# A two-layer encoder: the priorities of its list scheduler shifted by a table

## The chip, the cores and the metric

The kernel runs on one core of a Trainium2 chip. The core has five engines that run side by side: TensorE (PE, matmuls into PSUM), VectorE (DVE), ScalarE (ACT), GpSimd (POOL) and SyncE (SP, which here issues all DMAs). Each engine works through its own queue strictly in the order written in the program, and waits on semaphores for what the others must have finished. The metric is the device time of one execution in microseconds, lower is better.

## The reference

A bidirectional encoder trunk of two layers on a sequence of 512 tokens of width 1024, all in float32:

```python
h = layer_norm(x, ln_in_g, ln_in_b)
for l in range(2):
    proj = h @ w_in[l]                     # 1024 x 4608, split into nine parts
    # 4 heads of differential softmax attention, partial rotary
    a = softmax(q0 k0) - lam * softmax(q1 k1);  da = rms_norm(a @ v)
    # 4 heads of a gated linear recurrence, one scan per direction, summed
    hg = rms_norm(scan_fwd + scan_bwd) * silu(gate)
    # 4 heads of cross-attention into a memory of 256 tokens
    mx = softmax(q mk) @ mv
    h = layer_norm(alpha * h + concat(da, hg, mx) @ w_out[l])
    u = depthwise_conv3(h @ w_up[l])       # 1024 x 5632
    h = layer_norm(alpha * h + (silu(u_gate) * u_val) @ w_down[l])
```

## The kernel before, in words

**Matmuls in three halves.** Every large matmul is done in float16 with each operand split into a high and a low half: three matmuls per block (high x high, high x low, low x high), accumulated in float32 in PSUM. A weight block of 1 MB is loaded by a DMA, ScalarE squares and sums it (L307), a one-column matmul adds the sum over the partitions (L168, tile `stat`), VectorE makes a power of two from it (L155, L157, L159), ScalarE writes the scaled high half `wh` (L310) and VectorE the low half `wl` (L311). This chain runs 122 times.

**Stages of a layer.** The input projection (L140 is the one line of all matmuls) fills PSUM tiles `mm` (two buffers). Recurrence heads (`hg`) work through nine levels of block sizes: each level makes small matmuls into PSUM tiles `sc` (three buffers), copies them out under a mask on VectorE (L851, tile `hgD`), and multiplies queries and keys by products of the forget gates (L881 and L885). The differential attention (`da`) makes two score tiles in `sc`, takes their negative maximum (L1039, L1040), the exponential on ScalarE (L1042), their weighted difference (L1049 to L1051), and transposes it on TensorE (L513) into `tr` (two buffers). The output projection and the down projection add each finished PSUM block into the residual stream, which lies in four tiles z0 to z3 of 128 tokens (L569); this also frees the `mm` buffer. When a block of z is complete, its layer norm follows: statistics (L227, L229), an inverse root on GpSimd (L231, L232), scale and shift (L280, L281), transposes (L288) and a split into the halves `xh` and `xl` (L293). At the start the input is normalized block by block (L258), transposed (L262) and scaled by ScalarE (L264).

**What sets the order.** The program is built twice. The first time it is only recorded, as a list of 12099 operations with their engines. `extract` works out which operation depends on which. `deadlines` gives each a priority: for TensorE the place in the recorded order, in microseconds of TensorE work; for the others the latest moment at which they may end, worked back from those who need them. `simulate` then plays a list scheduler on modelled durations: an engine that is free takes, of the operations that are ready, the one with the lowest priority number. `make_plan` hands back the order of each engine and the buffer that each tile gets, and the second build writes exactly that order. So one number in the priorities can move many instructions on all engines, while what is computed stays as it was.

## Time and profile before

| what | value |
|---|---|
| time, median of 3 runs | 1492.83 us (1492.78 to 1493.38) |
| time of the profiled execution | 1492.88 us |
| its span, first to last instruction | 1491.1 us |
| instructions | 24496 |
| TensorE busy | 1451.7 us, 97% |
| VectorE busy | 1168.4 us, 78% |
| ScalarE busy | 865.1 us, 58% |
| GpSimd busy | 130.1 us, 9% |
| DMA moved | 141.91 MB, mean 95 GB/s |

Busy is the time in which an engine works on at least one instruction. The difference of a matmul engine's busy time from the span is what it lost. A wait is listed with the engine and line that ended it. L12 is line 12 of the kernel file; tile names in the profile stand without their numbers.

### The profile page before, as it was taken

To read this page: it belongs to the slowest core of one execution; us is meant where nothing else is said; L and a number is where in the kernel's file an instruction comes from. 1 tells how busy PE (TensorE), PEld (TensorE's weight loads), DVE (VectorE), ACT (ScalarE), POOL (GpSimd) and SP (SyncE) were. 2 spreads that over 40 slices of the span, in tenths; PEclk is the share of its full clock that TensorE was granted. 3 is DMA by queue.
4 is the path that set the end of the run, shared out by engine and by line. 5 is a ranking of instruction groups with operands and counts; after the bars stand their busy time and mean duration, and the time that the engine had idled before them with its cause. 6 is when DMAs were issued, how large, how long until landed. Compare 5 with 4: busy or idle time off the path is not lost. (4 is left out here: it accounts for less than half of the span.)

```text
span 1491.1 us, 24496 instructions
## 1 busy us (share of the span) xinstructions
PE 1451.7 (97%) x9978; PEld 811.9 (54%) x9978; DVE 1168.4 (78%) x2242; ACT 865.1 (58%) x1094; POOL 130.1 (9%) x154
## 2 busy tenths in 40 slices
PE   6999999999999999999999999999999999999997
PEld 4566675565564444444487475655656544444443
DVE  7989968978997677666785978789888777566777
ACT  5876655666376556455466656566645656455550
POOL 1001020000111101001000101001001101001011
PEclk9999999999999999999999999999999999999999
DMA  6342111223143323232324202112232323333221
GB/s 238 114 150 86 59 58 59 101 71 101 46 143 114 107 85 113 85 113 96 128 90 140 87 30 86 57 57 77 79 100 85 113 88 118 99 92 114 86 84 57
DMA packets 158171, 141.91 MB, mean 95 GB/s; under 512 B 3302, under 2 KB 139114, under 8 KB 158058
## 3 DMA queue, kind: packets, MB, share of 16 engines
q1 hardware_dynamic: 158058, 140.35, 29.2%
q8 instruction: 78, 1.28, 0.3%
q14 instruction: 35, 0.29, 0.1%
HBM read 138.24 MB, written 2.10 MB: 94 GB/s over the span
## 5 line engine op out<-in xcount | busy, mean ns | idle before, releaser
L140 PEld LDWEIGHTS <-wh 128*128 128x128 f16 x2624 | 251.0, 98 | 237.5 <-issue 3.4
L311 DVE SCALAR_TENSOR_TENSOR wl<-wst,ws,wh 128x2048 f16<-128x2048 f32 x122 | 312.5, 2561 | 52.3 <-ACT wh L310 51.4
L140 PE MATMUL mm<-xh,wl 128*128 128x512 f16 (+1 forms) x832 | 305.3, 367 | 0.6 <-DVE wl L311 0.6
L140 PE MATMUL mm<-xh,wh 128*128 128x512 f16 (+1 forms) x832 | 305.2, 367 | 0.0
L140 PE MATMUL mm<-xl,wh 128*128 128x512 f16 (+1 forms) x832 | 305.0, 367 | 0.0
L307 ACT ACTIVATE wh<-wst 128x2048 bf16<-128x2048 f32 x122 | 232.2, 1903 | 102.4 <-PE stat L168 49.2
L310 ACT ACTIVATE wh<-wst,ws 128x2048 f16<-128x2048 f32 x122 | 243.5, 1996 | 40.1 <-DVE ws L157 19.5
L140 PE MATMUL mm<-wh,t 128*128 128x512 f16 (+1 forms) x768 | 223.5, 370 | 0.0
L140 PEld LDWEIGHTS <-wl 128*128 128x128 f16 x1312 | 128.2, 98 | 123.0 <-DVE wl L311 0.9
L140 PEld LDWEIGHTS <-t 128*128 128x128 f16 x1152 | 110.2, 98 | 121.4 <-issue 0.6
L569 DVE SCALAR_TENSOR_TENSOR z<-mm,inv,z 128x512 f32<-128x512 f32 x176 | 130.2, 745 | 45.9 <-PE mm L140 32.2
L140 PE MATMUL sc<-xl,wh 128*128 128x512 f16 (+1 forms) x416 | 147.5, 355 | 0.0
L140 PE MATMUL sc<-xh,wl 128*128 128x512 f16 (+1 forms) x416 | 147.5, 355 | 0.0
L140 PE MATMUL sc<-xh,wh 128*128 128x512 f16 (+1 forms) x416 | 147.5, 355 | 0.0
L140 PE MATMUL mm<-wl,t 128*128 128x512 f16 (+1 forms) x384 | 142.1, 370 | 0.0
L155 DVE TENSOR_SCALAR we<-stat 128x1 int32<-128x1 int32 x122 | 18.6, 153 | 118.8 <-PE stat L168 118.6
L1151 POOL TENSOR_TENSOR t<-f 128x512 f32<-128x512 f32 x44 | 60.6, 1378 | 542.7 <-DVE f L1149 438.6
L140 PE MATMUL mm<-wh,mgh 128*128 128x512 f16 x192 | 73.3, 382 | 4.7 <-DVE z L569 4.7
L1147 ACT ACTIVATE f<-sc,cvb,cw 128x512 f32<-128x512 f32 x44 | 34.1, 775 | 71.4 <-PE stat L168 69.3
L140 PE MATMUL mm<-wh,mgl 128*128 128x512 f16 x192 | 72.9, 381 | 0.9 <-DVE mgl L547 0.6
L140 PE MATMUL mm<-wl,mgh 128*128 128x512 f16 x192 | 73.3, 382 | 0.0
L1042 ACT ACTIVATE f<-sc,dam,iqk 128x512 f32<-128x512 f32 x64 | 49.3, 774 | 38.8 <-DVE dam L1040 34.3
(244 smaller groups left out, 2125.4 us busy)
## 6 DMA issues: line engine op xcount, KB each, us to landing
wst<-in_w_up_dram SPq DMA_DIRECT2D x88, 512.0 KB, 4.3
wst<-in_w_in_dram SPq DMA_DIRECT2D x36, 1024.0 KB, 4.8
wst<-in_w_down_dram SPq DMA_DIRECT2D x22, 1024.0 KB, 4.9
wst<-in_w_out_dram SPq DMA_DIRECT2D x12, 1024.0 KB, 4.9
wst<-in_w_mem_kv_dram SPq DMA_DIRECT2D x8, 1024.0 KB, 5.0
z<-in_x_dram SPq DMA_DIRECT2D x4, 512.0 KB, 4.9
mix<-in_ln_g_dram SPq DMA_DIRECT2D x4, 512.0 KB, 3.6
mix<-in_ln_b_dram SPq DMA_DIRECT2D x4, 512.0 KB, 4.7
```

The source lines that it names most:

```text
L140: T.matmul(o, lhsT, rhs, start=start, stop=stop)
L155: V.tensor_scalar(e, tot.bitcast(I32), 0x7F000000, 1, ALU.bitwise_and, ALU.logical_shift_right)
L307: A.activation(h.rearrange("p a b -> p (a b)").bitcast(BF16), flat, AF.Square, accum_out=ss)
L310: A.activation(h.rearrange("p a b -> p (a b)"), flat, AF.Identity, scale=s)
L311: V.scalar_tensor_tensor(l.rearrange("p a b -> p (a b)"), flat, s, h.rearrange("p a b -> p (a b)"), ALU.mult, ALU.subtract)
L569: V.scalar_tensor_tensor(zs, p_, ivs[half % len(ivs)], zs, ALU.mult, ALU.add)
L1042: A.activation(pe[:, c, :], sc_[c], AF.Exp, bias=mx[:, c : c + 1], scale=iqk, accum_out=z1 if c else z0)
L1147: A.activation(c, p_, AF.Identity, scale=cw[:, 1, v : v + 1], bias=cvb[:, l, i + 22 * v : i + 22 * v + 1])
L1151: G.tensor_tensor(gt[:, n, :], c2[:, 0, :], c2[:, 1, :], ALU.mult)
```

## The change

No instruction of the kernel proper is edited. Three things change in the planner. `extract` now also orders two reads of one PSUM tile by the same engine (`soft` predecessors). `simulate` starts its model of the DMA queue at 2.1 us instead of 0. And the priorities get a table, `NUDGE`, of 335 rows (engine, first operation, last operation, shift in us), found by a local search over the planner's own model, with its durations as they are and with random changes to them; engine 0 is TensorE, 1 VectorE, 2 ScalarE, 3 GpSimd.

```diff
+                    elif psum and j != o.i and ops[j].eng == o.eng:
+                        o.soft.add(j)
...
+    for o in ops:
+        o.soft -= o.preds
+        o.preds |= o.soft
...
-    dma_free = 0.0
+    dma_free = 2.1
...
-            lat = LAT if ops[s].eng != o.eng else (0.03 if e != "PE" else -o.tail)
+            lat = LAT if ops[s].eng != o.eng else (0.03 if e != "PE" and i not in ops[s].soft else -o.tail)
...
+NUDGE = (
+    (1, 4476, 4542, -42.46), (0, 63, 66, -1.28), (0, 70, 261, 10.23), (0, 3136, 3180, 1.82), (1, 2922, 2934, 20.74), (1, 3035, 3050, -31.01),
...
+)
...
-    return [T[o.i] if o.eng == "PE" else D[o.i] for o in ops]
+    D = [T[o.i] if o.eng == "PE" else D[o.i] for o in ops]
+    for e, a, b, d in NUDGE:
+        for o in ops[a:b]:
+            if o.eng == ("PE", "DVE", "ACT", "POOL", "SP")[e]:
+                D[o.i] += d
+    return D
```

The counts of matmuls, vector and scalar operations and DMAs are the same. ScalarE's table of functions is loaded 9 times instead of 11. To turn one order into the other, at least 1530 of 8682 matmuls, 803 of 2226 VectorE, 210 of 829 ScalarE, 8 of 150 GpSimd operations and 4 of 212 DMAs have to move. Three places show what that looks like. The numbers in the names tell one buffer or tile from another.

**ScalarE, the first instructions.** Before:

```order
L307 ACTIVATE wh_12_131,wss_13_132<-wst_11_129 128x2048
L307 ACTIVATE wh_19_146,wss_20_147<-wst_18_144 128x2048
L264 ACTIVATE w2_38_200<-tr_37_195,gbc_88 128x512
L264 ACTIVATE w2_40_209<-tr_39_204,gbc_88 128x512
L310 ACTIVATE wh_12_131<-wst_11_129,ws_15_137 128x2048
L264 ACTIVATE w2_42_218<-tr_41_213,gbc_88 128x512
L264 ACTIVATE w2_44_227<-tr_43_222,gbc_88 128x512
L310 ACTIVATE wh_19_146<-wst_18_144,ws_22_152 128x2048
```

Now:

```order
L307 ACTIVATE wh_12_131,wss_13_132<-wst_11_129 128x2048
L264 ACTIVATE w2_38_200<-tr_37_195,gbc_88 128x512
L264 ACTIVATE w2_40_209<-tr_39_204,gbc_88 128x512
L310 ACTIVATE wh_12_131<-wst_11_129,ws_15_137 128x2048
L264 ACTIVATE w2_42_218<-tr_41_213,gbc_88 128x512
L264 ACTIVATE w2_44_227<-tr_43_222,gbc_88 128x512
L307 ACTIVATE wh_19_146,wss_20_147<-wst_18_144 128x2048
L264 ACTIVATE w2_46_236<-tr_45_231,gbc_88 128x512
```

The square of the second weight (`wh_19`) moved from second place to behind four of the L264; the high half of the first weight (`wh_12`, L310) comes one place earlier.

**VectorE, second layer, attention next to the output projection** (`wl_1966` is the low half of an output weight, the L569 add finished blocks into z). Before:

```order
L569 SCALAR_TENSOR_TENSOR z1_78<-mm_1981_11406,inv_1967_11346,z1_78 128x512
L1049 RECIPROCAL daz1_1926_11153<-daz1_1926_11153 128x1
L1050 SCALAR_TENSOR_TENSOR daz1_1926_11153<-daz1_1926_11153,nlam1_333,daz_1920_11136 128x1
L1039 TENSOR_REDUCE dam_1934_11180<-sc_1936_11182 128x1
L1039 TENSOR_REDUCE dam_1934_11180<-sc_1937_11183 128x1
L1051 SCALAR_TENSOR_TENSOR f4_1928_11155<-f4_1928_11155,daz1_1926_11153 128x512
L1040 TENSOR_SCALAR dam_1934_11180<-dam_1934_11180,iqk_1908_11065 128x2
L569 SCALAR_TENSOR_TENSOR z2_79<-mm_1988_11439,inv_1967_11346,z2_79 128x512
L311 SCALAR_TENSOR_TENSOR wl_1966_11343<-wst_1960_11331,ws_1964_11339,wh_1961_11333 128x2048
L569 SCALAR_TENSOR_TENSOR z3_80<-mm_1990_11456,inv_1967_11346,z3_80 128x512
L569 SCALAR_TENSOR_TENSOR z0_77<-mm_1999_11507,inv_1967_11346,z0_77 128x512
```

Now, the place to which the weight went:

```order
L311 SCALAR_TENSOR_TENSOR wl_1915_11079<-wst_1909_11067,ws_1913_11075,wh_1910_11069 128x2048
L1040 TENSOR_SCALAR dam_1922_11138<-dam_1922_11138,iqk_1908_11065 128x2
L311 SCALAR_TENSOR_TENSOR wl_1966_11343<-wst_1960_11331,ws_1964_11339,wh_1961_11333 128x2048
L1039 TENSOR_REDUCE dam_1927_11154<-sc_1930_11157 128x1
L1049 RECIPROCAL daz1_1921_11137<-daz1_1921_11137 128x1
L1039 TENSOR_REDUCE dam_1927_11154<-sc_1929_11156 128x1
L1050 SCALAR_TENSOR_TENSOR daz1_1921_11137<-daz1_1921_11137,nlam1_333,daz_1920_11136 128x1
```

and the place from which it went:

```order
L1039 TENSOR_REDUCE dam_1934_11180<-sc_1936_11182 128x1
L1051 SCALAR_TENSOR_TENSOR f4_1928_11155<-f4_1928_11155,daz1_1926_11153 128x512
L1039 TENSOR_REDUCE dam_1934_11180<-sc_1937_11183 128x1
L569 SCALAR_TENSOR_TENSOR z2_79<-mm_1988_11439,inv_1967_11346,z2_79 128x512
L1040 TENSOR_SCALAR dam_1934_11180<-dam_1934_11180,iqk_1908_11065 128x2
L569 SCALAR_TENSOR_TENSOR z3_80<-mm_1990_11456,inv_1967_11346,z3_80 128x512
L569 SCALAR_TENSOR_TENSOR z0_77<-mm_1999_11507,inv_1967_11346,z0_77 128x512
```

The L311 of `wl_1966` now follows the L311 of the weight before it, ahead of the score maxima of `dam_1927`, and no longer stands between the L569 of z2 and that of z3.

**VectorE, second layer, the layer norm after the output projection.** Before:

```order
L227 BN_STATS bnst_2072_11821<-z1_78 128x6
L191 SCALAR_TENSOR_TENSOR lnbd_2058_11750<-lnss_2053_11741 128x1
L229 BN_AGGR bnmv_2073_11824<-bnst_2072_11821 128x2
L192 TENSOR_SCALAR lnbd_2058_11750<-lnbd_2058_11750 128x1
L280 SCALAR_TENSOR_TENSOR z1_78<-z1_78,bnmv_2073_11824,mix_2054_11742 128x512
L155 TENSOR_SCALAR lne_2059_11753<-lnbd_2058_11750 128x1
L280 SCALAR_TENSOR_TENSOR z1_78<-z1_78,bnmv_2073_11824,mix_2054_11742 128x512
L157 TENSOR_SCALAR lns_2060_11755<-lne_2059_11753 128x1
L281 SCALAR_TENSOR_TENSOR z1_78<-z1_78,lnrs_2074_11826,mix_2056_11746 128x512
L194 COPY lnsc_81<-lns_2060_11755 128x1
L281 SCALAR_TENSOR_TENSOR z1_78<-z1_78,lnrs_2074_11826,mix_2056_11746 128x512
L569 SCALAR_TENSOR_TENSOR z2_79<-mm_2077_11847,inv_2040_11665,z2_79 128x512
```

Now:

```order
L569 SCALAR_TENSOR_TENSOR z1_78<-mm_2070_11805,inv_2062_11761,z1_78 128x512
L229 BN_AGGR bnmv_2066_11782<-bnst_2065_11779 128x2
L227 BN_STATS bnst_2072_11821<-z1_78 128x6
L280 SCALAR_TENSOR_TENSOR z0_77<-z0_77,bnmv_2066_11782,mix_2054_11742 128x512
L569 SCALAR_TENSOR_TENSOR z1_78<-mm_2071_11813,inv_2062_11761,z1_78 128x512
L280 SCALAR_TENSOR_TENSOR z0_77<-z0_77,bnmv_2066_11782,mix_2054_11742 128x512
L227 BN_STATS bnst_2072_11821<-z1_78 128x6
L569 SCALAR_TENSOR_TENSOR z2_79<-mm_2077_11847,inv_2040_11665,z2_79 128x512
L229 BN_AGGR bnmv_2073_11824<-bnst_2072_11821 128x2
L281 SCALAR_TENSOR_TENSOR z0_77<-z0_77,lnrs_2067_11784,mix_2056_11746 128x512
L280 SCALAR_TENSOR_TENSOR z1_78<-z1_78,bnmv_2073_11824,mix_2054_11742 128x512 x2
L281 SCALAR_TENSOR_TENSOR z1_78<-z1_78,lnrs_2074_11826,mix_2056_11746 128x512 x2
```

The L569 of z2 out of `mm_2077` moved from behind the normalization of z1 to ahead of it, and of the two L281 of z0 that stood ahead of these rows before, both stand behind it now.

## The prediction

> **What bounds the kernel now.** I read the page's totals first, then busy time by stretch, then who waits for whom on TensorE, then the order of time around the waits that cost most.

> ```profile
> span 1491.1 us, 24496 instructions
> PE 1451.7 (97%) x9978; PEld 811.9 (54%) x9978; DVE 1168.4 (78%) x2242; ACT 865.1 (58%) x1094; POOL 130.1 (9%) x154
> 1170.02 5.20 PE mm L140 x24
> ```

> TensorE (PE) is busy for 97% of the span. The third row, from the chain of waits, shows that this busy time is dense: 24 matmuls of 512 columns take 5.20 us, 0.217 us from start to start, and the change alters neither their number nor their shape. So the change can only give or take what TensorE loses between matmuls: 1491.1 - 1451.7 = 39.4 us. Where that lies, by stretch (us, then each engine's busy time):

> ```profile
> 0.00:25.00 25.00, 10.23 (x48) 7.50 (x49) 17.96 (x48) 13.49 (x15) 3.83 (x14) 1.00 0.75 271
> 75.00:180.00 105.00, 102.96 (x1382) 67.02 (x1381) 95.93 (x218) 70.62 (x91) 7.31 (x12) 1.00 0.32 104
> 260.00:410.00 150.00, 144.95 (x900) 83.73 (x898) 130.86 (x273) 85.90 (x137) 10.02 (x16) 1.00 0.24 79
> 825.00:925.00 100.00, 96.84 (x1437) 60.04 (x1436) 87.31 (x201) 57.93 (x89) 13.79 (x20) 1.00 0.23 75
> 1000.00:1150.00 150.00, 144.96 (x903) 86.44 (x900) 134.26 (x273) 88.17 (x134) 12.67 (x16) 0.99 0.24 78
> 1481.60:1491.10 9.50, 0.21 (x1) 0.00 (x0) 5.86 (x10) 0.00 (x0) 1.70 (x2) 0.68 0.29 110
> ```

> The first 25 us lose 14.8, the end after the last matmul 9.3, and four stretches in the middle 2.0 + 5.1 + 3.2 + 5.0 = 15.3. The other 952 us lose nothing. In those four stretches VectorE (DVE, the third busy column) is busy 87% to 91% of the time: there it is nearly as full as TensorE, and the order of its queue decides who waits. The waits of TensorE from 40 to 1480 us (total, times, longest):

> ```profile
> PE mm L140 <- DVE z L569: 4.7, 6, 2.7
> PE tr L513 <- DVE f L1051: 2.1, 2, 1.3
> PE sc L140 <- DVE hgD L851: 1.9, 5, 0.4
> PE sc L140 <- DVE t L881: 1.5, 4, 0.5
> ...
> PE tr L288 <- DVE z L281: 0.2, 1, 0.2
> ```

> These fifteen rows come to 14.8 us in 29 waits, nearly all on VectorE. L569, L851 and L1051 are short instructions (under 0.8 us) that free a PSUM buffer or finish an input. They come late because something longer or less urgent stands ahead of them in VectorE's strict order.

> **The change part by part.** No instruction of the mathematics is added or removed, so what is left is the place of each. Five terms follow. Gains are negative.

> *The wait at 1120 (second layer, layernorm).* The rows are in order of time for TensorE and then VectorE: start, duration, engine, line, operation; in brackets the idle time before it and who ended it.

> ```profile
> 1116.70 0.38 PE L140 MATMUL mm<-wh,mgl 128*128 128x512 f16 x1
> 1120.16 0.38 PE L140 MATMUL mm<-wh,mgl 128*128 128x512 f16 x1
> 1123.20 0.58 PE L140 MATMUL mm<-wh,mgh 128*128 128x512 f16 x1 [2.66 <-DVE z L569]
> 1114.80 0.73 DVE L569 SCALAR_TENSOR_TENSOR z<-mm,inv,z 128x512 f32<-128x512 f32 x1
> 1118.82 0.21 DVE L229 BATCH_NORM_AGGREGATE bnmv<-bnst 128x2 f32<-128x12 f32 x1
> 1121.01 0.75 DVE L281 SCALAR_TENSOR_TENSOR z<-z,lnrs,mix 128x512 f32<-128x512 f32 x1 [0.41 <-POOL lnrs L232]
> 1121.74 0.74 DVE L281 SCALAR_TENSOR_TENSOR z<-z,lnrs,mix 128x512 f32<-128x512 f32 x1
> 1122.40 0.74 DVE L569 SCALAR_TENSOR_TENSOR z<-mm,inv,z 128x512 f32<-128x512 f32 x1
> ```

> From start to start 3.04 us pass where 0.22 would do: 2.82 lost (the idle figure says 2.66, since the end of a matmul is modelled 0.16 later than the next could start; I add 0.16 to each wait below). The matmul waits for the L569 of z2, whose sum was ready with the matmul of 1116.70, but which stands behind the normalization of z1, which itself waited for GpSimd. In the new order it stands before L229 and the L281s. Ahead of it, after 1114.80, come that L569, two L280 and one batch statistic, four instructions of about 0.67 us: it can start at 1117.5 and end at 1118.2, before TensorE asks for it at about 1120. The 2.82 go. What is late next: one L281 of z0 now stands behind the normalization of z1, so the second group of transposes of z0 has its input at about 1123.1, while TensorE, no longer held, reaches them at about 1122.1 (1120.4 less the 0.44 of these transposes, which stood before that moment, and then ten matmuls of 0.22). That is a new wait of some 0.9. Term: -1.9, between -2.8 (no new wait) and -0.5.

> *The preparation of a weight taken away from in front of a release.* L311, the low half of a weight, is the longest instruction on VectorE.

> ```profile
> 1057.44 0.17 DVE L1049 RECIPROCAL daz<-daz 128x1 f32<-128x1 f32 x1 [1.70 <-ACT f L1042]
> 1064.85 2.34 DVE L311 SCALAR_TENSOR_TENSOR wl<-wst,ws,wh 128x2048 f16<-128x2048 f32 x1
> 1067.11 1.40 DVE L569 SCALAR_TENSOR_TENSOR z<-mm,inv,z 128x512 f32<-128x512 f32 x2
> 1067.91 0.38 PE L140 MATMUL mm<-wh,mgh 128*128 128x512 f16 x1 [0.45 <-DVE z L569]
> 1055.78 0.78 ACT L1042 ACTIVATE f<-sc,dam,iqk 128x512 f32<-128x512 f32 x1 [3.90 <-DVE dam L1040]
> ```

> Here the L311 of 2.34 us sits right ahead of the L569 for z3. In the new order it stands behind the previous L311, ahead of two softmax maxima, at about 1055.6: VectorE was idle there for 1.70 us, and ScalarE, which must first make the high half in 2.0 us, for 3.90. So it is paid out of two gaps, and if those gaps weren't there, it would delay the softmax by its 2.26 us instead. The same has happened, by the order, at the waits at 97.96, 172 and 173, 336 and 338, 1009, 1071: an L311 that stood one to eight places ahead is gone from there. The rows for L569 (without the 2.7 above), L1051 and L851 hold 2.0 + 2.1 + 1.9 = 6.0 us in 12 waits; with 0.16 each, 7.9. I take two thirds, -5.3; the ends are 0 and -7.9.

> *All other waits.* 14.8 - 2.7 - 6.0 = 6.1 us in 16 waits, 8.7 with 0.16 each. For about half of them the order shows more matmuls between the work that starts the chain and the one that waits (at 274, 344, 408, 1145), for the rest the same or fewer. -4.3, between 0 and -8.7.

> *The start.* In the new order ScalarE takes the square of the first weight, two L264, and then at once the L310 that the first matmul waits for; the square of the second weight goes behind it.

> ```profile
> 12.08 1.91 ACT L307 ACTIVATE wh<-wst 128x2048 bf16<-128x2048 f32 x1 [10.08 <-DMA wst<-in_w_in_dram]
> 14.80 1.91 ACT L307 ACTIVATE wh<-wst 128x2048 bf16<-128x2048 f32 x1 [0.72 <-DMA wst<-in_w_in_dram]
> 16.71 1.43 ACT L264 ACTIVATE w<-tr,gbc 128x512 f32<-128x512 f32 x2
> 18.03 1.99 ACT L310 ACTIVATE wh<-wst,ws 128x2048 f16<-128x2048 f32 x1
> 12.42 2.59 DVE L258 TENSOR_SCALAR z<-z,bnmv,lnrs 128x1024 f32<-128x1024 f32 x3
> 20.07 0.37 PE L140 MATMUL mm<-wh,xh 128*128 128x256 f16 x1 [0.59 <-ACT wh L310]
> 20.45 0.42 PE L140 MATMUL mm<-wh,xh 128*128 128x256 f16 x1
> 20.67 0.42 PE L140 MATMUL sc<-wh,xh 128*128 128x256 f16 x1
> 24.43 0.27 PE L140 MATMUL mm<-wh,xl 128*128 128x256 f16 x1
> 24.54 0.27 PE L140 MATMUL sc<-wh,xl 128*128 128x256 f16 x1
> ```

> The two L264 need the transposes of all four blocks of z, and so the last L258, which ends at 15.0. VectorE now does the statistics without the first L258 between them (0.80 us of the last three's 2.59 / 3 each moves behind), so the last ends near 14.7; with the scale columns after it the L264s run from about 15.4 to 16.8 and L310 to 18.8: the first matmul comes 1.2 earlier than at 20.07. But until about 24.1 matmuls of 256 columns follow each other in 0.22 us (20.45 to 20.67), later in 0.11 (24.43 to 24.54), although the granted clock of that stretch stands at 1.00. If the change of pace keeps its moment, half of the 1.2 is lost; if it comes after a fixed amount of work, all of it counts. -0.9, between 0 (the second weight is late instead) and -1.2.

> [...]

> *New waits.* 1530 of 8682 matmuls and 803 of 2226 VectorE instructions have changed places, and the new order also puts an L311 where none stood: five places ahead of the L851 that is waited for at 901, and two ahead of the L881 at 922. Each costs at most its 2.34, less what slack the matmuls between give. The lower end is 0. The upper end is that as much arises as goes, 12 us. I take +2.0, nearer to the low end, since only two of these are to be seen.

> The end of the kernel swaps the halves of the last block and keeps its length: 0. The two activation-table loads fewer, and one row swapped on the DMA queue here and there, lie on engines with slack: 0.

> **Sum:** -1.9 - 5.3 - 4.3 - 0.9 + 2.0 = -10.4. The profiled execution took 1492.88 us, 1.8 more than its span, and the median of the three runs is 1492.83, so nothing is to be corrected: 1492.9 - 10.4 = **1482.5 us**.

> **The rivals.**

> 1. *Waits only trade places.* VectorE is 87% to 91% full in the four stretches, and an instruction that goes forward pushes others back. Then new waits eat all but the start: 1492.9 - 0.9 = 1492.0. For it: a fuller engine cannot be made emptier. Against: the two places worked out above pay out of idle time. Chance 0.13.

> 2. *Weights pulled forward hold the queue up (slower).* VectorE works strictly in order. An L311 that stands earlier must find its high half done, else everything behind it waits for ScalarE's 1.99 us. If L311 are spread evenly, 122 x 505 / 1491 = 41 lie in the four stretches. If n of them hold the queue for 2.0 us each and the second term is lost, the change is -10.4 + 5.3 + 2.0 n: slower from n = 3 on, by more than a measurement's doubt from n = 5, and with n = 6, 1492.9 + 6.9 = 1499.8. For it: the two L311 newly near 901 and 922. Against: ScalarE's 3.90 idle before 1055.78 and its share of 58%. Chance 0.09.

> 3. *Nearly all waits go and none arises:* -2.8 - 7.9 - 8.7 - 1.2 = -20.6, 1472.3. Against: it needs durations on the chip to agree with the planner's to a few tenths of a microsecond in thousands of places. Chance 0.10.

> **How the numbers follow.** The forecast, with gains from 4 to 17 us, has 0.68. The range 1475.0 to 1492.5 takes its width and rival 1, and leaves out rivals 2 and 3, 0.19 together. The forecast's own range is 1475.9 to 1488.9. A measurement of this kernel can tell about 0.2%, 3 us, from no change. Faster: 0.68 + 0.10 + a little of rival 1 = 0.80. Within 0.2%: 0.11. Slower: 0.09.

> **What would show each step.** Idle of TensorE in the four stretches near 6 us where it was 15.3; no wait over 1 us around 1115, and perhaps one before a transpose of z; no L569 wait near 1060; the first L140 matmul at about 18.9; the time after the last matmul again 9 to 10 us. The prediction is wrong if the idle in the four stretches stays above 12, or if VectorE shows idle released by ScalarE's L310 ahead of L311.

## The result, and the profile after

| | kernel before | changed kernel |
|---|---|---|
| median time | 1492.80 us (1492.62 to 1493.38, 4 runs) | 1479.62 us (1479.27 to 1480.46, 4 runs) |
| ratio | | 0.9912, 95% interval 0.9895 to 0.9929 |
| profiled execution, its span | 1492.88 us, 1491.1 us | 1480.46 us, 1478.7 us |

The change makes the kernel 0.9% faster: 13.2 us between the medians, 12.4 us between the two profiled spans. The forecast was 10.4 us. The page of the changed kernel begins:

```profile
span 1478.7 us, 24479 instructions
PE 1446.2 (98%) x9978; PEld 812.7 (55%) x9978; DVE 1166.4 (79%) x2242; ACT 862.2 (58%) x1092; POOL 121.6 (8%) x154
```

The same 9978 matmul records keep TensorE busy for 1446.2 us where it was 1451.7. So 5.5 of the 12.4 us are not idle time at all; the busy time itself became shorter. The prediction had not foreseen that; where it lies is told below with the prediction's steps. Busy time by stretch (us, then the busy time of TensorE, its weight loads, VectorE, ScalarE and GpSimd, then the granted clock, DMA's share and GB/s):

```profile
0.00:25.00 25.00, 10.81 (x70) 9.45 (x71) 18.74 (x46) 13.13 (x17) 4.70 (x14) 1.00 0.81 295
75.00:180.00 105.00, 102.78 (x1370) 66.32 (x1368) 97.22 (x226) 70.74 (x91) 7.82 (x12) 1.00 0.30 100
260.00:410.00 150.00, 147.42 (x916) 85.96 (x915) 133.20 (x275) 85.38 (x135) 10.04 (x16) 0.99 0.25 81
825.00:925.00 100.00, 98.04 (x1397) 63.03 (x1396) 87.52 (x207) 58.90 (x90) 12.37 (x20) 1.00 0.22 73
1000.00:1150.00 150.00, 148.25 (x978) 93.39 (x977) 135.55 (x275) 91.19 (x136) 9.30 (x16) 1.00 0.26 85
1469.30:1478.70 9.40, 0.08 (x1) 0.00 (x0) 5.74 (x10) 0.00 (x0) 1.70 (x2) 0.79 0.30 112
```

The head still loses 14.2 us, the tail 9.3. The four stretches in the middle lose 2.2 + 2.6 + 2.0 + 1.7 = 8.5 where they lost 15.3. VectorE is as full there as before.

Idle time alone can mislead, since a matmul at half pace counts as busy: in the kernel before, TensorE is busy for 3.50 of the 3.50 us from 1123.20 on, at a granted clock of 0.51 (below). So I also compared the two traces at equal work. Every matmul got the usual distance from its start to the next start (the median of its shape in the trace before), and the loss up to a point is the time that has passed, less the sum of these distances. The sum over all matmuls is the same for both orders. Losses in us (a negative one means that the starts follow each other in less than these distances; the level of a part depends on which matmuls count as one shape, the differences hardly do):

| part of the program (time in the trace before) | before | after | difference |
|---|---|---|---|
| head, to 30 | 14.55 | 12.07 | -2.5 |
| first layer, attention and layernorm, 30 to 422 | 7.01 | 6.17 | -0.8 |
| first layer, feed-forward, 422 to 822 | 0.03 | 0.13 | +0.1 |
| second layer, recurrence, 822 to 972 | 10.35 | 8.31 | -2.0 |
| second layer, attention, 972 to 1110 | -1.59 | -4.55 | -3.0 |
| second layer, layernorm, 1110 to 1155 | 5.06 | 1.01 | -4.0 |
| rest | -0.16 | -0.32 | -0.2 |

The largest item is the wait at 1120. In the kernel before, by stretch:

```profile
1120.40:1123.20 2.80, 0.14 (x1) 0.00 (x0) 2.39 (x7) 1.26 (x2) 0.58 (x1) 1.00 0.00 0
1123.20:1126.70 3.50, 3.50 (x12) 2.19 (x12) 2.16 (x6) 0.69 (x1) 0.00 (x0) 0.51 0.00 0
1126.70:1130.00 3.30, 3.30 (x19) 1.68 (x18) 3.30 (x6) 0.69 (x1) 0.00 (x0) 1.00 0.00 0
```

Behind the wait the granted clock is 0.51 for 3.5 us. From start to start the matmuls of 512 columns there take 0.43 us, where it is 0.22 from 1126.82 on, which costs another 1.6 us on top of the 2.82 that the wait costs. TensorE was busy all through it, so no table of waits shows it. In the changed kernel this place has one wait of 0.84 us and keeps its clock (1112.80 to 1114.02, quoted at the third experiment). But in this profile the changed kernel has a half clock in another place, behind short waits of 0.55, 0.77, 0.65 and 0.36 us between 341 and 345:

```profile
341.20:344.60 3.40, 1.19 (x8) 0.66 (x6) 3.35 (x12) 3.40 (x6) 0.00 (x0) 1.00 0.02 7
344.60:348.10 3.50, 3.38 (x12) 1.28 (x13) 2.84 (x7) 3.04 (x5) 0.00 (x0) 0.54 0.33 102
348.10:351.50 3.40, 3.40 (x30) 3.31 (x30) 3.28 (x5) 0.87 (x2) 0.00 (x0) 0.97 0.19 65
```

What TensorE waits for now, 40 to 1467 us (total, times, longest; 16 rows, 8.4 us in 18 waits, where it was 14.8 in 29):

```profile
PE sc L140 <- issue: 1.5, 1, 1.5
PE tr L513 <- DVE f L1051: 0.9, 2, 0.6
PE mm L140 <- DVE z L569: 0.8, 1, 0.8
...
PE tr L470 <- DVE ge L155: 0.8, 1, 0.8
...
PE sc L140 <- DVE hgD L851: 0.4, 1, 0.4
...
PE tr L513 <- DVE w L528: 0.2, 1, 0.2
```

The three kinds that the second term named (L569, L851, L1051) are nearly gone. The first row is new: a gap that nothing in the profile released (experiments 10 and 11).

### The profile page after: what moved, and what is told of

Read it like the earlier page. It is cut to its first block, busy times and chain, and to the rows that moved or that the text cites. A ratio compares the mean times of both kernels' runs of the same rounds, so it can differ in the third digit from the quotient of the medians.

```text
span 1478.7 us, 24479 instructions
## 1 busy us (share of the span) xinstructions
PE 1446.2 (98%) x9978; PEld 812.7 (55%) x9978; DVE 1166.4 (79%) x2242; ACT 862.2 (58%) x1092; POOL 121.6 (8%) x154
## 4 chain that ended last, share of the span: by engine, by line
PE 87%; DVE 8%; ACT 2%; issue 1%; POOL 0%; DMA 0%; SPq 0%; POOLq 0%; DVEq 0%; ACTq 0%
PE mm L140 59%; PE sc L140 20%; PE tr L140 5%; DVE t L881 1%; DVE t L885 1%; PE tr L513 1%; DVE wl L311 1%; ACT wh L310 1%; PE tr L288 1%; ACT wh L307 1%; PE tr L968 0%; DVE z L569 0%; DVE hgD L851 0%; DVE bnst L227 0%; ACT t L862 0%
## 5 line engine op out<-in xcount | busy, mean ns | idle before, releaser
L140 PEld LDWEIGHTS <-wh 128*128 128x128 f16 x2624 | 251.0, 98 | 235.9 <-issue 2.5
L311 DVE SCALAR_TENSOR_TENSOR wl<-wst,ws,wh 128x2048 f16<-128x2048 f32 x122 | 306.0, 2510 | 59.5 <-ACT wh L310 59.1
L140 PE MATMUL mm<-xl,wh 128*128 128x512 f16 (+1 forms) x832 | 303.6, 367 | 0.0
L140 PE MATMUL mm<-xh,wl 128*128 128x512 f16 (+1 forms) x832 | 303.6, 367 | 0.0
L140 PE MATMUL mm<-xh,wh 128*128 128x512 f16 (+1 forms) x832 | 303.4, 367 | 0.2
L307 ACT ACTIVATE wh<-wst 128x2048 bf16<-128x2048 f32 x122 | 232.2, 1903 | 110.9 <-PE mm L140 67.8
L310 ACT ACTIVATE wh<-wst,ws 128x2048 f16<-128x2048 f32 x122 | 243.2, 1996 | 70.1 <-DVE wi L159 49.6
L140 PE MATMUL mm<-wh,t 128*128 128x512 f16 (+1 forms) x768 | 225.8, 370 | 0.0
L140 PEld LDWEIGHTS <-wl 128*128 128x128 f16 x1312 | 128.1, 98 | 123.7 <-issue 2.4
L140 PEld LDWEIGHTS <-t 128*128 128x128 f16 x1152 | 110.7, 98 | 121.8 <-DVE f L1149 0.2
L569 DVE SCALAR_TENSOR_TENSOR z<-mm,inv,z 128x512 f32<-128x512 f32 x176 | 130.9, 746 | 51.3 <-PE mm L140 41.4
L140 PE MATMUL sc<-xh,wh 128*128 128x512 f16 (+1 forms) x416 | 147.2, 354 | 0.0
L140 PE MATMUL sc<-xl,wh 128*128 128x512 f16 (+1 forms) x416 | 147.2, 354 | 0.0
L140 PE MATMUL sc<-xh,wl 128*128 128x512 f16 (+1 forms) x416 | 146.9, 354 | 0.0
L140 PE MATMUL mm<-wl,t 128*128 128x512 f16 (+1 forms) x384 | 142.1, 370 | 0.0
L140 PE MATMUL mm<-wh,mgh 128*128 128x512 f16 x192 | 73.0, 381 | 1.2 <-DVE z L569 0.8
L140 PE MATMUL mm<-wl,mgh 128*128 128x512 f16 x192 | 73.2, 381 | 0.0
L140 PE MATMUL mm<-wh,mgl 128*128 128x512 f16 x192 | 72.5, 380 | 0.1
L1042 ACT ACTIVATE f<-sc,dam,iqk 128x512 f32<-128x512 f32 x64 | 49.3, 775 | 30.4 <-DVE dam L1040 26.3
```

Source lines behind the costliest of these rows:

```text
L140: T.matmul(o, lhsT, rhs, start=start, stop=stop)
L307: A.activation(h.rearrange("p a b -> p (a b)").bitcast(BF16), flat, AF.Square, accum_out=ss)
L310: A.activation(h.rearrange("p a b -> p (a b)"), flat, AF.Identity, scale=s)
L311: V.scalar_tensor_tensor(l.rearrange("p a b -> p (a b)"), flat, s, h.rearrange("p a b -> p (a b)"), ALU.mult, ALU.subtract)
L569: V.scalar_tensor_tensor(zs, p_, ivs[half % len(ivs)], zs, ALU.mult, ALU.add)
L1042: A.activation(pe[:, c, :], sc_[c], AF.Exp, bias=mx[:, c : c + 1], scale=iqk, accum_out=z1 if c else z0)
```

## The experiments

**1. The planner's two edits without the table.**

```diff
-NUDGE = (
-    (1, 4476, 4542, -42.46), ...
-)
+NUDGE = ()
```

> The changed kernel with its table of shifts emptied; the two edits to the planner's rules (same-engine PSUM order kept, the data path starting 2.1 us late) stay. Table theory: the table carries the gain, so this falls back to the kernel before, 1490 to 1494 us. Rival: the rules carry a part of it that can be measured, 1489 us or less. In the trace the L569 wait of 2.7 us that stood near 1120 is back under the table theory.

Measured: 1491.99 us median, ratio to before 0.9996 (0.9986 to 1.0005). The loss at the layernorm of the second layer is back at 4.9 us, and the wait for L569 there at 2.65. So the table carries the gain, and the two edits of the rules none that can be measured.

**2. The table without the rows of the first layer.**

```diff
     for e, a, b, d in NUDGE:
+        if 300 <= a < 5900:
+            continue
```

> The changed kernel without the rows of the table for operations 300 to 5899 (the first layer's attention and most of its feed-forward). Theory from the two traces: the loss of TensorE at equal work differs by 2.5 us after the first 25 us and by 3.2 before the second layer, so all these rows together bring 0.7 us: 1480.3 us, between 1479.3 and 1482. Rival, the prediction's own second and third term: the places at 98, 172, 274, 336, 344 and 408 bring about half of 9.6 us, so 1484.4 us.

Measured: 1482.49 us (1482.30 to 1482.69), 2.9 above the changed kernel, between the two numbers and above the range of the first. At equal work this kernel loses 7.9 us between 30 and 422 us, the changed one 6.2: 1.8 us for these 174 of 335 rows. The second profile of the changed kernel (experiment 11) loses only 3.7 there, which would make it 4.2; so the size is known to no better than that. In the second layer the losses of each part agree with the changed kernel to 0.1 us. So a shift in one part of the program stays in that part; between the two layers lies a feed-forward in which TensorE hardly waits.

**3. Only the L569 that TensorE waits for at 1120 is moved, in the kernel before.**

```diff
+    seq = order["DVE"]
+    seq.remove(9674)
+    seq.insert(seq.index(9643), 9674)
```

> The kernel before with a single instruction moved: on VectorE the L569 of z2 out of mm_2077 stands ahead of the batch statistics of z1 (L229) and not behind its normalization. Prediction's first term: -1.9 (-2.8 to -0.5), 1490.9 us, with a new wait of about 0.9 before the second transposes of z0. Theory from the trace after: the whole loss between 1100 and 1135 falls from 4.7 to about 1.0, so -3.7, 1489.1 us. Rival, waits only trade places: 1492.8 us.

Measured: 1493.15 us (1491.63 to 1493.8, 10 runs), ratio 1.0003 (0.9993 to 1.0012): no gain. The trace says why, in order of time, for TensorE and then VectorE:

```profile
1120.99 0.38 PE L140 MATMUL mm<-wh,mgh 128*128 128x512 f16 x1
1124.00 0.66 PE L288 MATMUL tr<-cst,z 128*128 128x128 f32 x4 [2.63 <-DVE xl L293]
...
1123.20 1.41 DVE L293 SCALAR_TENSOR_TENSOR xl<-tr,lnsc,xh 128x512 f16<-128x512 f32 x2 [0.16 <-ACT xh L292]
```

The matmul no longer waits for L569, and four matmuls later TensorE waits just as long. The transposes of z1 need a `tr` buffer, which the L293 of z0 frees, and that L293 stands behind the same normalization of z1. The rival, waits only trade places, holds at this place for a single move. In this one profile the clock did not fall behind the wait (1.00 from 1124.0 to 1127.5; the loss is 3.5 and not 4.7); experiment 11 says why. But nine of the ten runs took 0.9 to 2.2 us longer than the profiled one. Their mean granted clock is 0.996 where that of the profiled one is 0.998, so it fell somewhere in them; that it was here was not seen.

In the changed kernel the transposes of z1 stand 26 matmuls later, and in that place is only this wait, for the L569 of a later block:

```profile
1112.80 0.38 PE L140 MATMUL mm<-wh,mgl 128*128 128x512 f16 x1
1114.02 0.38 PE L140 MATMUL mm<-wh,mgh 128*128 128x512 f16 x1 [0.84 <-DVE z L569]
```

**4. The head: one L307 put back on ScalarE, in the changed kernel.**

```diff
+    seq = order["ACT"]
+    seq.remove(32)
+    seq.insert(seq.index(67), 32)
```

> The changed kernel with one instruction put back: on ScalarE the L307 of the second weight stands again ahead of the first two L264. Clock theory: the first L140 matmul goes back to about 20.1 (18.55 now) and the slow pace of the matmuls ends near 24.0 and not at 20.6, so +2.5 us, 1482.1. Rival, the pace changes after a fixed moment or not with this: only the first matmul moves, the slow pace still ends at 20.6, +0.9 to +1.5 us, 1480.5 to 1481.1.

Measured: 1481.28 us, 1.7 above the changed kernel. The first L140 matmul is back at 20.24. But the slow pace ends at 21.1, neither at 24.0 nor at 20.6, so both theories missed. Over the profiles it ended at 24.1 (before), 24.1 (experiment 3), 21.2 (experiment 1), 21.1 (here), 20.6 (changed) and 20.0 (experiment 2), with the first L140 matmul at 20.1, 20.2, 20.1, 20.2, 18.6 and 18.9. Neither a fixed moment nor a fixed distance from the first L140 matmul fits. At equal work the head loses 13.4 us here, 12.1 in the changed kernel, and in the kernel before 14.6 where the pace changed late and 13.6 (experiment 1, nearly the same order) where it changed early. So the move on ScalarE is worth about 1.3 us, and about 1 us between the two profiles is chance: it is the moment at which the pace changed (experiment 5).

**5. Matmuls on constants before the head, in the changed kernel.** For this and the next ones a filler stands in front of one named operation on TensorE:

```diff
-        return slot(pp, [P, 512], F32, tag, ...)
+        return filled(T, ones, f"{tag}_{counter[0] + 1}", slot(pp, [P, 512], F32, tag, ...))
...
+FILL = {'tr_37': (100, 63)}
+
+def filled(T, ones, name, t):
+    for _ in range(FILL.get(name, (0, 0))[0]):
+        T.matmul(t[:, 0:P], ones, ones, start=True, stop=True)
+    return t
```

> The changed kernel with 100 extra matmuls of 128 columns on constants, on TensorE between 4.3 us and the first transpose at 13.4, where it has nothing to do; their result is overwritten. Clock theory: TensorE is at full pace when the real work comes, the transposes from 13.4 on follow each other in 0.11 us and not 0.21, the first L140 matmul comes at about 18.1 (18.55), and none of the L140 matmuls is at 0.22: -1.4 us, 1478.2. Rival, the pace depends on what is busy in the stretch itself: the same slow stretch to about 20 to 24 us, 1479.6.

Measured: 1480.77 us, not faster (1.2 above). By stretches of 3.4 us:

```profile
4.70:8.10 3.40, 3.40 (x34) 3.40 (x33) 2.70 (x7) 0.00 (x0) 0.79 (x2) 1.00 1.01 382
8.10:11.50 3.40, 3.40 (x64) 3.40 (x62) 2.40 (x7) 0.00 (x0) 0.88 (x3) 1.00 1.05 382
11.50:14.90 3.40, 0.86 (x11) 0.69 (x8) 3.33 (x8) 1.85 (x2) 2.60 (x4) 1.00 1.10 400
14.90:18.30 3.40, 2.75 (x14) 2.16 (x13) 2.75 (x13) 2.76 (x5) 0.00 (x0) 0.51 1.04 384
18.30:21.80 3.50, 2.91 (x14) 2.33 (x13) 3.16 (x4) 3.50 (x4) 0.00 (x0) 0.50 0.41 164
21.80:25.20 3.40, 3.40 (x33) 3.17 (x33) 3.40 (x8) 3.33 (x8) 0.00 (x0) 1.00 0.75 257
```

**6. Matmuls on constants in the waits at 341 to 345, in the changed kernel.**

```diff
+FILL = {'tr_625': (12, 2862), 'tr_714': (15, 3242), 'mm_777': (8, 3431)}
```

> The changed kernel with 35 extra matmuls of 128 columns on constants in the three waits of TensorE at 341.1, 341.9 and 344.2 (12, 15 and 8 of them, 0.056 us each); their result is overwritten. Clock theory: the granted clock stays at 1.00 from 344 to 348 where it fell to 0.61, and the matmuls of 512 columns keep 0.22 us and not 0.43: -1.7 us, 1477.9. Rival, VectorE sets the pace there and TensorE only waits longer elsewhere: 1479.6. If the extra matmuls are late themselves: up to 1480.5.

Measured: 1479.57 us, no difference that can be told from the changed kernel's 1479.62 (four runs each). The trace of it, by stretch:

```profile
341.00:345.00 4.00, 3.30 (x47) 2.68 (x47) 3.57 (x11) 4.00 (x8) 0.00 (x0) 1.00 0.00 0
345.00:348.50 3.50, 3.12 (x23) 1.70 (x21) 3.50 (x7) 3.06 (x5) 0.00 (x0) 1.00 0.16 45
```

The clock stays at 1.00, as the clock theory says, and the loss at this place falls from 1.4 to 0.4: 1.0 and not 1.7, since the fillers are themselves a little late. In this profile the head happened to lose 0.8 more, so that little of it is left in the span (1478.2).

**7. Matmuls on constants in the wait at 1120, in the kernel before.**

```diff
+FILL = {'sc_2110': (45, 9688)}
```

> The kernel before with 45 extra matmuls of 128 columns on constants in the 3 us wait at 1120.4 (ahead of the matmul that waits for the L569 of z2); their result is overwritten. No instruction moves on VectorE. Clock theory: the wait stays as long as it is (2.8 us), but the granted clock of 0.51 from 1123.2 to 1126.7 goes back to 1.00 and 1.6 us are saved: 1491.1 us. Rival, VectorE is the bound there, and what TensorE gains it waits for at the next transposes: 1492.7 us.

Measured: 1492.50 us, ratio 0.9998 (0.9988 to 1.0007). In the profile, in order of time:

```profile
1120.43 2.67 PE L1675 MATMUL sc<-ones 128*128 128x128 bf16 x45
1123.25 0.38 PE L140 MATMUL mm<-wh,mgh 128*128 128x512 f16 x1
```

and by stretch:

```profile
1120.00:1124.00 4.00, 3.86 (x52) 3.13 (x51) 3.59 (x8) 1.27 (x2) 1.00 (x1) 1.00 0.02 4
1124.00:1127.50 3.50, 3.50 (x23) 2.21 (x22) 3.42 (x8) 1.34 (x2) 0.00 (x0) 1.00 0.00 0
```

The wait ends where it ended, no instruction moved, and the clock stays at 1.00 where it was 0.51. The loss of the place goes from 4.7 to 3.4, as in experiment 3. So 1.3 of the 4.7 belonged to the clock alone, and 3.4 stay while VectorE's order stays. In the median 0.4 us of it shows, less than the runs differ.

**8. One weight put back, in the changed kernel.**

```diff
+    seq = order["DVE"]
+    seq.remove(9270)
+    seq.insert(seq.index(9364), 9270)
```

> The changed kernel with a single instruction put back on VectorE: the L311 of 2.34 us for wl_1966 stands again right ahead of the L569 of z3 (mm_1990), and not 10 us earlier behind the other L311. Prediction's second term at this place: a wait of 0.6 us of TensorE for L569 comes back, 1480.2 us. Upper end, its whole length: 2.3 us, 1481.9. Rival, slack on both sides takes it up: 1479.6 us.

Measured: 1481.30 us (1480.46 to 1481.59), 1.7 above the changed kernel. At equal work the loss of this part rises by 1.1 us, and that of no other part changes by more than 0.3. The wait comes back where the second term had it (TensorE's waits, 1040 to 1070):

```profile
PE mm L140 <- DVE z L569: 0.8, 2, 0.6
```

In the changed kernel L569 has no row in that stretch. The mechanism of the second term is shown at this place: 0.8, and 0.16 for each of two waits, is 1.1.

**9. Only the 19 rows of the table around the second layer's layernorm.**

```diff
     for e, a, b, d in NUDGE:
+        if not 9400 <= a < 10400:
+            continue
```

> The changed kernel with only those 19 of the 335 rows of the table that touch operations 9400 to 10399 (the end of the second layer's attention and its layernorm). Theory from the trace after: order is made locally, so the place at 1100 to 1135 comes out as in the changed kernel (loss 1.0 us and not 4.6, no half clock) while the rest stays as with the empty table: 1492.0 - 3.6 = 1488.4 us. Rival: the place needs the rows before it, or the wait only trades places as it did when one L569 was moved: 1490.8 to 1492 us.

Measured: 1489.55 us, ratio 0.9979 (0.9969 to 0.9988). The loss at 1110 to 1155 is 1.0 as in the changed kernel (4.9 with the empty table), with one wait of 0.84 for L569, and 0.7 us more are lost just ahead of it. So 19 rows, of which ten move VectorE's order, five TensorE's and four ScalarE's, do what the single move of experiment 3 could not, and they need nothing from the rest of the table. Which of them are needed was not tested. The median moved by 2.4 against the empty table, 1.2 less than forecast; the spans of the two profiles by 3.4.

**10. Three places at once, in the changed kernel.**

```diff
+FILL = {'tr_37': (115, 63), 'tr_41': (10, 77), 'mm_76': (14, 172), 'tr_625': (12, 2862), 'tr_714': (15, 3242), 'mm_777': (8, 3431)}
...
+    seq = order["PE"]
+    for k in (1008, 953, 954, 955):
+        seq.remove(k)
+    at = seq.index(907)
+    seq[at:at] = [1008, 953, 954, 955]
```

> The changed kernel with three edits. (1) Extra matmuls on constants at the head: 115 of them up to the first transpose, 10 and 14 in the two gaps up to the first L140 matmul. (2) The 35 extra matmuls at 341 to 344. (3) Four matmuls of 512 columns moved between the two bursts of 64 small matmuls at 92.9. Clock theory for (1): the clock no longer falls at the head, the loss of the first 25 us goes from 12.1 to about 10.5. For (2): the loss there 1.4 to 0.4, as measured before. For (3), if the gap of 1.65 us without a releaser comes from instructions that arrive too slowly in a long burst: 3.1 to about 1.6. Sum -4.1: 1475.5 us. Rival: (1) gives nothing and (3) only moves the gap: 1478.6.

Measured: 1478.61 us (1478.16 to 1478.91, 4 runs), ratio to before 0.9906 (0.9891 to 0.9921). It is the lowest median of all, and experiments 11 and 12 ask what that is worth. Read place by place: (1) the clock never falls at the head, and the loss there is 12.0, the same as without the fillers. The first L140 matmul is at 18.59: ScalarE's L310 sets it. Of what TensorE gains behind it, one wait of 0.25 us for VectorE's L266 takes a part; the rest was not taken apart. The rival was right on the head. (2) 1.4 to 0.4, as before. (3) The loss around 93 goes from 3.1 to 1.4, and 0.7 of it comes back a little later: 1.0 is left. The gap that (3) is about, in the changed kernel:

```profile
92.66 0.45 PE L140 MATMUL sc<-t,w 128*32 128x32 f32 x29
94.56 0.58 PE L140 MATMUL sc<-t,w 128*32 128x32 f32 x35 [1.46 <-issue]
```

It lies in the middle of a burst of small matmuls, at an instruction that waits for no semaphore. With the burst broken in two by four large matmuls, no wait without a releaser is left.

**11 and 12. The changed kernel once more, and beside it the tenth without the fillers of the head.**

> The changed kernel as it is, timed beside the next one for a direct comparison: 1479.3 to 1480.5 us, as before.

> As the kernel with three places filled, but without the extra matmuls at the head: the 35 extra matmuls at 341 to 344 and the four matmuls moved between the two bursts at 93. Theory from the traces: 1.0 us from each, and the head gives nothing, so 1.0 to 2.0 us under the changed kernel run beside it, 1478.6 or less. Rival, VectorE takes the gain back and the lower median before was chance or the head's: the same as the changed kernel, 1479.6.

Measured: the changed kernel 1480.06 us (1478.46 to 1480.91, 4 runs; ratio 0.9915, 0.99 to 0.993), the other 1479.16 us (1478.50 to 1479.59, 4 runs; 0.9911, 0.9895 to 0.9928). So 0.9 us, just under what the theory allowed, and inside the spread of the changed kernel. Why that spread exists shows in the second profile of the changed kernel, 1478.46 us and 1476.7 us of span, by the stretches that had the half clock in the first one:

```profile
341.20:344.60 3.40, 1.54 (x9) 0.77 (x10) 3.35 (x11) 3.40 (x6) 0.00 (x0) 1.00 0.04 11
344.60:348.10 3.50, 3.50 (x28) 2.49 (x25) 3.50 (x5) 2.47 (x4) 0.00 (x0) 1.00 0.36 133
```

The same instructions, in the same order, with the same waits, and the clock does not fall: the loss of this place is 0.0 where it was 1.4. The burst at 93 shows no stop either:

```profile
93.09 0.46 PE L140 MATMUL sc<-t,w 128*32 128x32 f32 x32
93.71 0.46 PE L140 MATMUL sc<-t,w 128*32 128x32 f32 x32 [0.16 <-PE sc L140]
```

Everything from 350 us on agrees with the first profile to 0.1 us. So the half clock at 344 and the gap at 93 are draws of each execution, together about 2 us.

For the clock, the grid of experiment 5 shows what differs between the two. In the first profile a window runs from 341.46 to 344.87 us, and TensorE is busy for 1.24 us of it. In the second the windows end at 342.50 and 345.91, so the same waits are split over two, with 2.09 and 2.41. Between 25 and 1460 us of all fourteen profiles the clock fell behind each of the nine windows with 1.63 us of work or less, and behind none with 1.65 or more. In the kernel before, the window ahead of 1123.20 has 0.76; in experiment 3 the wait of 2.63 us is split over windows with 1.65 and 2.55, and the clock holds. As far as these profiles show, for the clock only where the grid lies differs between executions.

Experiments 6, 10 and 12 take the draw away: their best runs (1479.08, 1478.16, 1478.50) are about the best of the changed kernel (1478.46). That a version with fillers is faster than the changed kernel is not shown: the medians are 0.1 (experiment 6), 1.0 (10) and 0.9 us (12) lower, and the intervals overlap almost wholly. What stops a burst now and then was not found.

## Why the prediction was right, and where it was not

The sign, the size and the range hold: 13.2 us against 10.4, 1479.62 in 1475.9 to 1488.9. The sum is right by terms that were off in both directions; that they cancel is luck.

| term | predicted | measured (traces) |
|---|---|---|
| 1 the wait at 1120 | -1.9 | -4.0 (loss 5.06 to 1.01) |
| 2 waits for L569, L1051, L851 elsewhere | -5.3 | -6.1 (6.0 in 12 waits to 1.3 in 3, and 0.16 for each) |
| 3 and 5 other waits and new ones | -4.3 + 2.0 | -0.1 (6.1 in 16 to 6.3 in 14, and 0.16 for each) |
| 4 the start | -0.9 | -2.5 |
| not in the sum: the half clock at 344 | 0 | +1.4 (first profile against second, experiment 11) |
| sum | -10.4 | -11.3, of 12.4 between the spans |

*The first step* let only the idle time of TensorE change. Its busy time fell by 5.5 us as well: 1.9 at the head and 2.1 at the second layer's layernorm, where the slow clock is shorter or gone, with 1.2 more in the first layer, where this profile of the kernel before has no slow clock, and 2.8 less elsewhere. Each wait also counts 0.16 us of a modelled end as busy; the 11 that are gone make up to 1.8 of that.

*Term 1* fails in its second step, "what is late next". A wait of 0.9 for the second transposes of z0 was forecast. Experiment 3 shows that the next to wait are the transposes of z1, for 2.63 us, and that moving L569 alone saves nothing. In the changed kernel these transposes stand behind 26 more matmuls, and the wait that is left is for another L569. That its 0.84 has the forecast's size is chance. The 19 rows of experiment 9 give it all; they move TensorE, VectorE and ScalarE, and TensorE's move alone was not tested. The term was also mis-sized. It priced the wait at 2.82, and 1.3 to 1.6 us more lay in the half clock behind it (experiment 7), which was there in the profiles of the kernel before and of experiment 1 and not behind the like wait of experiment 3, which the grid splits (experiment 11). The sign of that stood in the prediction's own rows: the last stretch but one showed a clock of 0.99 where the other stretches in the middle had 1.00.

*Term 2* is the one that held best. A low half of a weight in front of a release costs what the row says, tested at one place by undoing it (experiment 8: 1.1, forecast 0.6 there). The other places were not tested.

*Terms 3 and 5.* About half of the other waits should have gone; as many came as went. The first row of the waits after, 1.5 us without a releaser, is a quarter of it; experiment 11 shows that it is not there in every execution. The half clock at 344, which no term has, is not the change's doing: with the empty table (experiment 1) the clock falls at 345.45 too.

*Term 4.* The first matmul came at 18.55, forecast 18.9, so the order on ScalarE did what it was to do (1.3 us by experiment 4). The rest is the moment at which the clock changes. The prediction asked whether that moment stays or follows the work. In the fourteen profiles it lies on the grid of experiment 5, at the end of the first window with 2.82 us of work or more, so it came earlier with earlier work, and by where the grid lay it differed by 2.9 us between nearly the same orders (24.1 in the kernel before, 21.2 in experiment 1). With the old order on ScalarE it came at 21.1 to 24.2 us in six profiles, with the new one at 19.6 to 21.7 in six (without those that fill the head), and the head lost 14.0 and 12.4 us on average. So about 1.6 of the 2.5 us belong to the change, more than the term's end of 1.2, and the rest to the grid. Between these two profiles the change of pace came 3.5 us earlier (24.11 to 20.60).

*What was to be seen.* Idle in the four stretches: 8.5, forecast near 6, with 12 as the limit. Around 1115 no wait over 1 us: 0.84. No L569 wait near 1060: none. Tail 9 to 10: 9.3. The last mark, idle of VectorE that ScalarE's L310 ends ahead of L311, was to speak for rival 2. As it is worded the kernel before met it already:

```profile
L311 DVE SCALAR_TENSOR_TENSOR wl<-wst,ws,wh 128x2048 f16<-128x2048 f32 x122 | 312.5, 2561 | 52.3 <-ACT wh L310 51.4
```

and in the changed one:

```profile
L311 DVE SCALAR_TENSOR_TENSOR wl<-wst,ws,wh 128x2048 f16<-128x2048 f32 x122 | 306.0, 2510 | 59.5 <-ACT wh L310 59.1
```

It rose by 7.7 us, and TensorE has no row for it: VectorE had that time to spare.

*Rivals.* The first, waits only trade places, came true at 1120 for a single move. In the first layer it only looked so: the two profiles differ by 0.8 us there, but without its 174 rows the kernel takes 2.4 to 2.9 us more (experiment 2 against the two timings of the changed kernel). The other two did not come.

## What to carry to other kernels

Before a wait is priced, look at the granted clock behind it: here one wait of 2.66 us (1120, kernel before) and several of 0.36 to 0.77 us close together (341 to 345, changed kernel) were each followed by 3.4 us at half clock in the profiled execution, which cost 1.3 to 1.6 us more at 1120 and 1.4 at 344, and that part counts as busy. When an instruction that someone waits for is moved ahead, follow the buffer that the next consumer needs as well; here moving the one instruction alone saved nothing (experiment 3), and the rows that also move those consumers did (experiment 9). And this scheduler's shifts acted locally (experiments 2 and 9), so a table of hundreds of rows could be taken apart by stages: 19 of its 335 rows bring 2.4 of some 12 us.

## What the runs showed of the hardware that was not expected

- The clock fell without an empty window: between 341.2 and 344.6 TensorE was busy for 1.19 of 3.40 us, with no single wait over 0.9 us, and the next 3.5 us ran at 0.54. In another execution of the same program, with 1.54 us of work in the same stretch, it stayed at 1.00 (experiment 11). Laid on the grid of 3.413 us, from 25 to 1460 us of the fourteen profiles, the clock fell behind all nine windows with up to 1.63 us of work and behind none with 1.65 or more; the slow clock, at the head and later, ended behind the 24 windows with 2.82 us or more. The ends of matmuls are modelled, so these limits are those of these traces.
- The times of one kernel spread by 0.4 to 2.5 us, part of it for this reason, and a single profile is a draw: two profiles of the changed kernel differ by 2.0 us, at two places. Extra matmuls on constants in the waits held the clock at 1.00 there (experiments 6, 7, 10, 12).
- A run of 64 small matmuls (128x32) stopped in its middle, with 0.6 to 1.5 us of idle time, at an instruction that waits for nothing the profile shows: in the burst at 93 us in five of six profiles that hold this order (not in experiment 11), and twice at other places (908 in experiment 4, 829 in experiment 5).
